# Down projection of a gated MLP as seven products of 2x2 blocks, with the sums of its weight blocks made ahead, in a one-core trunk kernel

## The chip, the cores and the metric

The kernel runs on one core of a Trainium2 chip. The metric is device time in microseconds (us) for one execution of the whole program. Five engines work side by side, each through its own queue, strictly in the queue's order: TensorE (PE in the profile; weight loads of the array are PEld), VectorE (DVE), ScalarE (ACT), GpSimd (POOL) and SyncE (SP), which here only issues DMAs. ACT issues a few DMAs too. An instruction waits at the head of its queue until the engines it depends on have signalled.

## What is computed

One decoder layer on x of 2048 tokens by 1024 channels, in float32: a token mixer of four head groups, then a gated channel mixer. The change lies in the channel mixer, which ends the program:

```python
D_MODEL, SEQ, D_FF = 1024, 2048, 2816
...
up, gate = split(rmsnorm(x, pre2) @ w_up)            # 1024 -> 2 x 2816
gate = causal_depthwise_conv(gate, width 3) + bias   # over tokens
h = gelu_tanh(gate) * up                             # 2048 x 2816, F in the kernel
out = x + rmsnorm(h @ w_down, post2)                 # 2816 -> 1024
```

(The names are shortened; the function is the reference's.) Float32 products are made of float16 ones: each operand is scaled by a power of two and split into a high and a low float16 part, and a product takes three matmuls, high by high, high by low and low by high.

## The kernel before

The stage in question is `stage_n` and, called from its end, `ffn_down`. P = 128 partitions, C = 512 columns, NF = 22 tiles of 128 hidden channels, NC = 4 blocks of 512 tokens, NSUB = 4 blocks of 128 tokens in each.

**Up projection.** `ffn_up(p, j, w)` makes hidden tile j for the pair p of token blocks (p = 0: tokens 0 to 1023, p = 1: the rest). It already uses seven products of 2x2 blocks (L1672, 7 x 12 = 84 matmuls of 128x512), with the outputs put together on ACT and DVE (L1675, L1685, L1689). The convolution and GELU follow on ACT and DVE (L1705 to L1708), the multiplication by `up` on POOL (L1709), and the tile goes to DRAM as `fD` (L1710). Its largest magnitude is taken on DVE (L1711, `mF`) in the *next* call, as `late`. Tiles are taken in the order (0, j), (1, j), (0, j+1), ..., and the built program interleaves neighbouring calls.

The weights of tile j+1 are prepared while tile j is multiplied. `up_weights` loads 1 MB (`raw`), takes the largest magnitude on DVE, spreads it over the partitions with an all-reduce on POOL (L1625), and makes the four differences and sums of blocks on POOL (L1626). `up_split` computes the scale on DVE (L220 to L222, L1649) and writes the high part on ACT (L1652) and the low part on DVE (L1653) into `Wup`. `down_max` reads tile j of the down weights (512 KB, `rd`) only to take its largest magnitude (`mD`, L1638).

**Between the projections.** `f_scale(p)` finds the scale of pair p's F with one all-reduce on POOL (L1723); for p = 0 the scale of the down weights comes from the same one.

**Down projection.** For the first block of 512 tokens, every hidden tile j loads its weights again (`weights`, 512 KB on ACT's DMA queue, L1751), splits them on ACT and DVE (L1753, L1754) into `Wd`, which then stays in SBUF, loads and splits F (`values`, L1759 to L1762) and adds 8 x 3 matmuls of 128x512 (L1768) into eight PSUM banks. The other three blocks go by 128 tokens, with two banks each. `out` scales, normalises, adds x and stores.

The order in each queue is fixed when the program is built, by a scheduler that lists instructions by priority; `issue_after` moves a group of instructions behind a given one.

Of the kernel before, what the change touches and what calls it, by code (L numbers as in the profile page):

```python
# [97 lines left out]
def _layout(inp):  # L98
# [41 lines left out]
class Trunk:  # L140
# [1430 lines left out]
    def stage_n(self):  # L1571
# [3 lines left out]
        self.fD = self.dram.tile([NF, P, T], F32, name="fD")  # L1575
        with ExitStack() as ctx:
            self.small = self.sn
            self.Wt.append(self.pool(ctx, "n_w").tile([P, 2, 7, C], F16, name="Wup1"))
# [3 lines left out]
            self.up, self.gb, self.F = two("up", [P, 2, C]), two("gb", [P, 2 * C + 2]), two("F", [P, 2, C])  # L1582
            self.rd = one("rd", [P, D])
# [72 lines left out]
    def ffn_up(self, p, j, w):  # L1656
# [57 lines left out]
    def f_scale(self, p, mark):

        nc, small = self.nc, self.sn
        self.small = small
        n = 2 if p else 3
        mm = small.tile([P, 6], F32, name="mm", bufs=2)
        nc.vector.tensor_reduce(out=mm[:, 0:2], in_=self.mF[:, 2 * p:2 * p + 2], axis=AX.X, op=ALU.max)  # L1720
        if p == 0:
            nc.vector.tensor_reduce(out=mm[:, 2:3], in_=self.mD, axis=AX.X, op=ALU.max)
        nc.gpsimd.partition_all_reduce(mm[:, 3:3 + n], mm[:, 0:n], P, RMAX)  # L1723
        with self.tc.issue_after(mark.ins):
            un, sc = self.pow2(mm[:, 3:3 + n], 14)
            if p == 0:
                nc.vector.tensor_copy(out=self.sd[:, 0:1], in_=un[:, 2:3])
                nc.vector.tensor_copy(out=self.sd[:, 1:2], in_=sc[:, 2:3])
            nc.vector.tensor_scalar(out=self.sf[:, 2 * p:2 * p + 2, 0], in0=un[:, 0:2], scalar1=self.sd[:, 0:1], scalar2=None, op0=ALU.mult)
            nc.vector.tensor_copy(out=self.sf[:, 2 * p:2 * p + 2, 1], in_=sc[:, 0:2])  # L1730

    def ffn_down(self):

        nc = self.nc
        with ExitStack() as ctx:
            wa = self.pool(ctx, "wa_d")
            Wd = [None] * 3 + [wa.tile([P, 2, D], F16, name=f"Wd{j}") for j in range(3, 18)]
            s0 = self.pool(ctx, "s0_d")
            early = [s0.tile([P, D], F32, name="wdr0"), s0.tile([P, 2, C], F32, name="fr0"), s0.tile([P, 3, 2, C], F16, name="f0")]
            wb = self.pool(ctx, "wb_d")  # L1740
            st = self.pool(ctx, "st_d", bufs=4)
            fp = self.pool(ctx, "f_d")
            self.row(fp, "post2")
# [3 lines left out]
            Wd = [wb.tile([P, 2, D], F16, name=f"Wd{j}") for j in range(3)] + Wd[3:] + [wb.tile([P, 2, D], F16, name=f"Wd{j}") for j in range(18, NF)]  # L1747

            def weights(j):
                r = early[0] if j < 3 else st.tile([P, D], F32, name="wdr", bufs=3)  # L1750
                nc.scalar.dma_start(out=r, in_=self.A["w_dn"][j])  # L1751
                W = Wd[j]
                nc.scalar.activation(out=W[:, 0], in_=r, func=AF.Copy, scale=sd[:, 1:2])  # L1753
                self.mark = nc.vector.scalar_tensor_tensor(out=W[:, 1], in0=r, scalar=sd[:, 1:2], in1=W[:, 0], op0=ALU.mult, op1=ALU.subtract)  # L1754

            def values(c, j):
                e = c == 0 and j < 3
                r = early[1][:, j % 2] if e else st.tile([P, C], F32, name="fr")
                nc.sync.dma_start(out=r, in_=self.fD[j][:, c * C:(c + 1) * C])  # L1759
                f = early[2][:, j] if e else fp.tile([P, 2, C], F16, name="f", bufs=NF + 5)  # L1760
                nc.scalar.activation(out=f[:, 0], in_=r, func=AF.Copy, scale=sf[:, c, 1:2])
                nc.vector.scalar_tensor_tensor(out=f[:, 1], in0=r, scalar=sf[:, c, 1:2], in1=f[:, 0], op0=ALU.mult, op1=ALU.subtract)  # L1762
                return f

            def mms(ps, f, i, n, j):
                sl, ns = slice(i * P, (i + 1) * P), slice(n * C, (n + 1) * C)
                for k, (a, b) in enumerate(((0, 0), (0, 1), (1, 0))):
                    nc.tensor.matmul(ps, lhsT=f[:, a, sl], rhs=Wd[j][:, b, ns], start=j == 0 and k == 0, stop=j == NF - 1 and k == 2)  # L1768

            def out(c, i, ps):  # L1770
                r = slice(c * C + i * P, c * C + (i + 1) * P)
                x = fp.tile([P, D], F32, name="xo", bufs=3)
                nc.scalar.dma_start(out=x, in_=self.x2[r])
                o = fp.tile([P, D], F32, name="od", bufs=2)
                nc.scalar.activation(out=o[:, 0:C], in_=ps[0], func=AF.Copy, scale=sf[:, c, 0:1])
                nc.vector.tensor_scalar(out=o[:, C:], in0=ps[1], scalar1=sf[:, c, 0:1], scalar2=None, op0=ALU.mult)  # L1776
                jk = fp.tile([P, D], BF16, name="jk", bufs=1)
                ss = small.tile([P, 2], F32, name="nss")
                nc.scalar.activation(out=jk, in_=o, func=AF.Square, accum_out=ss[:, 0:1])
                self.small = small  # L1780
                self.rsqrt(ss[:, 1:2], ss[:, 0:1], 1.0 / D, EPS)
# [6 lines left out]
            for j in range(NF):  # L1788
                weights(j)
                f = values(0, j)  # L1790
                if j == 8:
                    self.f_scale(1, self.mark)
                for i in range(NSUB):
                    for n in range(2):
                        mms(ps[i][n], f, i, n, j)
# [37 lines left out]
```

## Time and profile before

| | |
|---|---|
| median of 3 runs | 3024.64 us (3021.18 to 3032.18) |
| the profiled execution | 3021.11 us, span 3019.3 us, mean granted clock 0.943 |
| PE busy | 2746.7 us, 91% of the span |
| DVE, ACT, POOL busy | 1726.0, 1038.3, 802.9 us (57%, 34%, 27%) |
| up stage, steady, one hidden tile j (168 matmuls) | 36.69 us |
| last matmul of the up projection ends | 2528.3 us |
| first matmul of the down projection | 2542.55 us |
| down projection | 2112 matmuls |

The span runs from the first to the last instruction that the profile shows; the profiled execution's own time is 1.8 us longer. Busy shares are averages over the program; a stage is read from its own rows. A row of a timeline gives start, duration, engine, line and operation, and in brackets how long the engine had been idle and what released it.

### The profile page before, as it was taken

How to read it: one execution, taken by the hardware profiler on the slowest of the kernel's cores; microseconds unless marked ns; L12 is line 12 of the kernel's file. 1: busy time of each engine (PE TensorE's matmuls, PEld its weight loads, DVE VectorE, ACT ScalarE, POOL GpSimd, SP SyncE). 2: the span in 40 equal slices, each digit the busy share in tenths (PEclk: the TensorE clock that was granted, in tenths of full speed). 3: DMA queues.
4: the chain of work that ended last, by engine and by line, in shares of the span. 5: the costliest groups of instructions: out<-in, count | busy, mean ns of one | idle time of the engine just before them, and what ended most of it. 6: DMA issues, size and time to landing. Idle time of an engine off the chain costs nothing.

```text
span 3019.3 us, 45043 instructions
## 1 busy us (share of the span) xinstructions
PE 2746.7 (91%) x17401; PEld 1655.2 (55%) x17401; DVE 1726.0 (57%) x3517; ACT 1038.3 (34%) x1844; POOL 802.9 (27%) x979
## 2 busy tenths in 40 slices
PE   5998998999978997899966779999999997999998
PEld 2455776777757885676744424444444443444443
DVE  7645674767766554677864566666666665513021
ACT  5433222444532224466662322222233223412020
POOL 2432221323333331123333332322222221010110
PEclk9998998999988998899987989999999998999999
DMA  9522333345543384574433311122111214623120
GB/s 264 123 62 79 87 92 96 93 103 139 132 113 85 93 218 152 133 169 125 121 85 92 91 56 63 70 74 73 70 70 70 72 70 158 213 91 105 42 87 22
DMA packets 341400, 313.70 MB, mean 104 GB/s; under 512 B 217600, under 2 KB 271232, under 8 KB 338368
## 3 DMA queue, kind: packets, MB, share of 16 engines
q1 hardware_dynamic: 265856, 238.42, 27.9%
q10 hardware_dynamic: 75328, 72.39, 8.1%
q8 instruction: 137, 2.24, 0.3%
q14 instruction: 79, 0.65, 0.1%
HBM read 187.86 MB, written 89.56 MB: 92 GB/s over the span
## 4 chain that ended last, share of the span: by engine, by line
PE 61%; DVE 14%; issue 9%; DMA 7%; ACT 4%; POOL 3%; SPq 1%; ACTq 0%; POOLq 0%; DVEq 0%
PE psd L1768 10%; PE psb L1672 9%; PE psc L1672 5%; PE psa L1672 5%; PE psf L298 2%; PE psf L299 2%; PE psf L300 2%; DVE Wup L1653 2%; PE psf L308 1%; PE psf L310 1%; PE psf L309 1%; PE psb L662 1%; PE pss L1253 1%; PE pso L1415 1%; PE psb L682 1%
## 5 line engine op out<-in xcount | busy, mean ns | idle before, releaser
L1672 PEld LDWEIGHTS <-Wup 128*128 128x128 f16 x3696 | 362.8, 99 | 518.0 <-issue 61.2
L1768 PE MATMUL psd<-Wd,f 128*128 128x512 f16 x2112 | 460.9, 381 | 20.9 <-ACT Wd L1753 20.0
L1768 PEld LDWEIGHTS <-f 128*128 128x128 f16 x2112 | 207.6, 98 | 274.2 <-issue 19.1
L1672 PE MATMUL psa<-V,Wup 128*128 128x512 f16 x1056 | 254.7, 385 | 34.2 <-ACT Wup L1652 17.0
L1672 PE MATMUL psb<-T,Wup 128*128 128x512 f16 x792 | 189.7, 382 | 17.9 <-ACT T L1567 13.5
L1675 DVE SCALAR_TENSOR_TENSOR up<-psb,wm,X 128x512 f32<-128x512 f32 x88 | 65.9, 749 | 214.4 <-PE psb L1672 214.2
L308 PE MATMUL psg<-Wo,yt 128*128 128x256 f16 x512 | 145.4, 284 | 29.8 <-DMA yt<-hl 25.2
L1685 ACT ACTIVATE X<-psa,wm 128x512 f32<-128x512 f32 x44 | 30.2, 687 | 389.0 <-DVE up L1675 387.2
L298 PE MATMUL psf<-U,hi_fm 128*128 128x256 f16 x576 | 162.4, 282 | 0.0
L299 PE MATMUL psf<-U,hi_fm 128*128 128x256 f16 x576 | 162.3, 282 | 0.0
L300 PE MATMUL psf<-U,lo_fm 128*128 128x256 f16 x576 | 162.0, 281 | 0.0
L310 PE MATMUL psg<-Wo,yt 128*128 128x256 f16 x512 | 144.3, 284 | 5.4 <-DMA yt<-hl 5.4
L309 PE MATMUL psg<-Wo,yt 128*128 128x256 f16 x512 | 145.4, 284 | 0.0
L1776 DVE TENSOR_SCALAR od<-psd,sf 128x512 f32<-128x512 f32 x16 | 12.0, 750 | 232.0 <-PE psd L1768 227.5
L308 PE MATMUL psf<-hi_fv,U 128*128 128x256 f16 (+1 forms) x512 | 136.2, 275 | 1.4 <-DVE gt L873 1.4
L309 PE MATMUL psf<-lo_fv,U 128*128 128x256 f16 (+1 forms) x512 | 136.1, 274 | 1.1 <-DVE lo_fv L286 1.1
L310 PE MATMUL psf<-hi_fv,U 128*128 128x256 f16 (+1 forms) x512 | 136.5, 274 | 0.0
L1371 DVE TENSOR_REDUCE fmx<-psf 128x1 f32<-128x512 f32 (+3 forms) x160 | 95.8, 606 | 56.3 <-PE psf L1368 39.9
L1709 POOL TENSOR_TENSOR F<-F,up 128x1024 f32<-128x1024 f32 x44 | 103.8, 2359 | 81.4 <-ACT F L1708 74.1
L1672 PE MATMUL psc<-V,Wup 128*128 128x512 f16 x528 | 121.1, 379 | 0.0
L1405 ACT ACTIVATE fP<-psf,ln2k 128x512 f32<-128x512 f32 (+3 forms) x160 | 98.3, 626 | 65.6 <-PE psf L1403 26.6
L1415 PE MATMUL pso<-FV,fhl 128*128 128x129 f16 x1088 | 99.8, 227 | 15.3 <-POOL fhl L1409 7.6
(458 smaller groups left out, 6157.7 us busy)
## 6 DMA issues: line engine op xcount, KB each, us to landing
raw<-in_w_up SPq DMA_DIRECT2D x22, 1024.0 KB
fD<-F SPq DMA_DIRECT2D x44, 512.0 KB
fr<-fD SPq DMA_DIRECT2D x88, 256.0 KB
rd<-in_w_dn SPq DMA_DIRECT2D x22, 512.0 KB
wdr<-in_w_dn ACTq DMA_DIRECT2D x22, 512.0 KB
zin<-zR SPq DMA_DIRECT2D x80, 128.0 KB
ka<-kA ACTq DMA_DIRECT2D x40, 256.0 KB
wst<-in_w_cm SPq DMA_DIRECT2D x17, 512.0 KB
```

What stands on the lines that cost most here:

```text
L298: nc.tensor.matmul(ps[:, sl], lhsT=hi[:, k, n0:n0 + nn], rhs=uh[:, k, sl], start=k == 0, stop=False)
L299: nc.tensor.matmul(ps[:, sl], lhsT=hi[:, k, n0:n0 + nn], rhs=ul[:, k, sl], start=False, stop=False)
L300: nc.tensor.matmul(ps[:, sl], lhsT=lo[:, k, n0:n0 + nn], rhs=uh[:, k, sl], start=False, stop=k == KT - 1)
L308: nc.tensor.matmul(ps, lhsT=uh[:, k, sl], rhs=hi[:, k, n0:n0 + nn], start=k == 0, stop=False)
L309: nc.tensor.matmul(ps, lhsT=uh[:, k, sl], rhs=lo[:, k, n0:n0 + nn], start=False, stop=False)
L310: nc.tensor.matmul(ps, lhsT=ul[:, k, sl], rhs=hi[:, k, n0:n0 + nn], start=False, stop=k == KT - 1)
L1371: nc.vector.tensor_reduce(out=mx[:, i, b:b + 1], in_=ps[:, :n], axis=AX.X, op=ALU.min)
L1405: nc.scalar.activation(out=e[:, o:], in_=ps[:, o:], func=AF.Exp, scale=-1.0, bias=self.ln2k)
L1415: nc.tensor.matmul(po[i // 2][:, i % 2 * 129:i % 2 * 129 + 129], lhsT=h[:, n, i * P:(i + 1) * P], rhs=self.V2[:, s, hp], start=s == 0 and ...
L1672: nc.tensor.matmul(ps, lhsT=W[:, a, n, ks], rhs=rhs[u](b, k), start=first and k == 0 and i == 0, stop=k == 3 and i == 2, skip_group_check= ...
L1709: nc.gpsimd.tensor_tensor(out=t, in0=t, in1=up.rearrange("p c n -> p (c n)"), op=ALU.mult)
L1768: nc.tensor.matmul(ps, lhsT=f[:, a, sl], rhs=Wd[j][:, b, ns], start=j == 0 and k == 0, stop=j == NF - 1 and k == 2)
```

## The change

The down projection is written as seven products of 2x2 blocks as well: the hidden tiles are paired (j with j + 11), the two halves of the 1024 output columns, and the two token blocks of a pair p. A step (p, i, j) takes 128 tokens of each block of the pair, seven combinations of F and seven of the weights, and 7 x 3 = 21 matmuls into seven PSUM banks. There are 2 x 4 x 11 = 88 steps. `out` adds the seven banks up into four quarters.

- `down_max` becomes `down_sums`: for each of the 11 pairs it loads 1 MB of down weights, takes the largest magnitude, makes four differences on POOL in place and stores them to DRAM as `dT`. It is called 11 times, with the tiles j = 4 to 14 of the up stage, after `ffn_up(1, j)`.
- `d_scale`, with an all-reduce of its own, takes over the down weights' scale; `f_scale` keeps one scale for the pair.
- F goes to `fD` in two stores of 256 KB, laid out by 128-token blocks.
- The last `ffn_up` calls change places: (0, 20), (0, 21), (1, 20), (1, 21).
- `weights(j)` loads 0.75 MB of `w_dn` and 1 MB of `dT`, on SP's queue, into two buffers or into the space of `Wd8`, `Wd9`, `Wd10`. `values` loads F for one step into `X`, makes four 128x128 sums on POOL, and splits the 896 columns on ACT and DVE into `O`. Both run three steps ahead of the matmuls, the first three steps in memory that the first pair's up projection has left.

```diff
     def down_sums(self, j, mark):
+        d = self.rd
+        nc.sync.dma_start(out=d.rearrange("p s n -> p (s n)"), in_=self.A["w_dn"][j])
         with self.tc.issue_after(mark.ins):
-            nc.vector.tensor_reduce(out=self.mD[:, j:j + 1], in_=d, axis=AX.X, op=ALU.max, apply_absolute_value=True)
+            nc.vector.tensor_reduce(out=self.mD[:, j:j + 1], in_=d.rearrange("p s n -> p (s n)"), axis=AX.X, op=ALU.max, apply_absolute_value=True)
+        for o, a, b in ((1, 0, 1), (0, 3, 0), (3, 3, 1), (2, 3, 2)):
+            nc.gpsimd.tensor_tensor(out=d[:, o], in0=d[:, a], in1=d[:, b], op=ALU.subtract)
+        nc.sync.dma_start(out=self.dT[j], in_=d)
...
     def stage_n(self):
-            for j in range(2, NF):
...
+            for j in range(2, NF - 1):
+                W[j + 1] = self.up_weights(j + 1)
                 mark = self.ffn_up(0, j, W[j])
+                W[j + 1] = self.up_split(j + 1, W[j + 1], mark)
+                if j < NF - 2:
+                    mark = self.ffn_up(1, j, W[j])
+                    if 4 <= j < 4 + NF // 2:
+                        self.down_sums(j - 4, mark)
+                    if j == 5 + NF // 2:
+                        self.d_scale(mark)
+            self.ffn_up(0, NF - 1, W[NF - 1])
+            self.f_scale(0, self.ffn_up(1, NF - 2, W[NF - 2]))
+            self.ffn_up(1, NF - 1, W[NF - 1])
             self.late()
...
+    def d_scale(self, mark):
+        nc.vector.tensor_reduce(out=mm[:, 0:1], in_=self.mD, axis=AX.X, op=ALU.max)
+        nc.gpsimd.partition_all_reduce(mm[:, 1:2], mm[:, 0:1], P, RMAX)
...
     def ffn_down(self):
+            def weights(j):
+                r, W = raw[(0, 1, 0, 2, 3, 0, 1, 2, 0, 1, 0)[j]], Wd[j]
+                nc.sync.dma_start(out=r[0], in_=self.A["w_dn"][j][:, C:].rearrange("p (s n) -> p s n", s=3))
+                nc.sync.dma_start(out=r[1], in_=self.dT[j])
+                for o, x in ((slice(0, 3), r[0]), (slice(3, 7), r[1])):
+                    nc.scalar.activation(out=W[:, 0, o], in_=x, func=AF.Copy, scale=sd[:, 1:2])
+                    self.mark = nc.vector.scalar_tensor_tensor(out=W[:, 1, o], in0=x, scalar=sd[:, 1:2], in1=W[:, 0, o], op0=ALU.mult, op1=ALU.subtract)
+
+            def values(n, p, i, j):
+                x, o = X[n % 3], O[n % 4]
+                nc.sync.dma_start(out=x[:, 0:4].rearrange("p (h s) t -> p h (s t)", h=2), in_=self.fD[:, j, :, p, i].rearrange("h p n -> p h n"))
+                for d, a, b, op in ((4, 0, 2, ALU.add), (5, 4, 1, ALU.subtract), (6, 1, 0, ALU.subtract), (7, 3, 5, ALU.subtract)):
+                    nc.gpsimd.tensor_tensor(out=x[:, d], in0=x[:, a], in1=x[:, b], op=op)
+                nc.scalar.activation(out=o[:, 0], in_=x[:, 1:8], func=AF.Copy, scale=sf[:, p, 1:2])
+                nc.vector.scalar_tensor_tensor(out=o[:, 1], in0=x[:, 1:8], scalar=sf[:, p, 1:2], in1=o[:, 0], op0=ALU.mult, op1=ALU.subtract)
+                return o
...
+            for n in range(lead):
+                prepare(n)
+            for n, (p, i, j) in enumerate(steps):
+                prepare(n + lead)
...
+                for b, (a, w) in zip(ps, ((0, 0), (4, 6), (2, 1), (5, 3), (3, 4), (6, 2), (1, 5))):
+                    for k, (x, y) in enumerate(((0, 0), (0, 1), (1, 0))):
+                        nc.tensor.matmul(b, lhsT=o[:, x, a], rhs=W[:, y, w], start=j == 0 and k == 0, stop=j == H - 1 and k == 2)
+                if j == H - 1:
+                    out(p, i, ps)
```

POOL's queue in one step of the up stage before: the block sums of the next up weights, and F's multiplication behind them (ISA rows are the all-reduce and the switches of POOL's library on either side of it).

```order
L1626 TENSOR_TENSOR S<-raw 128x512
L1625 ISA
L1625 ISA wm<-wm 128x1
L1626 ISA
L1626 TENSOR_TENSOR raw<-raw 128x512
L1626 TENSOR_TENSOR S<-raw 128x512
L1626 TENSOR_TENSOR S<-raw,S 128x512
L1709 TENSOR_TENSOR F_19222<-F_19222,up_19206 128x1024
```

POOL's queue after the change: the end of the same step with `down_sums`, and the later step in which `d_scale` falls (L1716 is F's multiplication, L1644 the four differences, L1728 the all-reduce of `d_scale`).

```order
L1629 TENSOR_TENSOR S<-raw,S 128x512
L1644 TENSOR_TENSOR rd<-rd 128x512 x4
L1716 TENSOR_TENSOR F_19237<-F_19237,up_19229 128x1024
...
L1629 TENSOR_TENSOR S<-raw,S 128x512
L1644 TENSOR_TENSOR rd<-rd 128x512
L1728 ISA
L1728 ISA md<-md 128x1
L1644 ISA
L1644 TENSOR_TENSOR rd<-rd 128x512 x3
L1716 TENSOR_TENSOR F_19237<-F_19237,up_19229 128x1024
```

In each of these steps four differences, and once an all-reduce with two library switches, have come between the block sums and F's multiplication. The two rows of calls behind F's multiplication are as before.

DVE's queue at the same place, after the change; the names and their order are those of before (L1719 was L1711, L1660 was L1653).

```order
L1682 SCALAR_TENSOR_TENSOR up_19221<-psb,wm,X 128x512
L1719 TENSOR_REDUCE mF<-F_19237 128x2
L221 TENSOR_SCALAR p_1_22658<-wm 128x1
L1682 SCALAR_TENSOR_TENSOR gb_19225<-psb,wm,X 128x512
L222 TENSOR_SCALAR p_1_22658<-p_1_22658 128x1
L1682 SCALAR_TENSOR_TENSOR gb_19217<-psc,wm,gb_19217 128x512
L223 RECIPROCAL p_1_22658<-p_1_22658 128x1
L1656 TENSOR_TENSOR wm<-p_1_22658,ug 128x1
L1713 SCALAR_TENSOR_TENSOR F_19233<-gb_19217,pc,F_19233 128x1024
L1714 SCALAR_TENSOR_TENSOR F_19233<-gb_19217,pc,F_19233 128x1024
L1660 SCALAR_TENSOR_TENSOR Wup_19209<-raw,p_1_22658,Wup_19209 128x2048
```

Nothing moved here: the maximum of F stands where it stood, ahead of the scale and the split of the next up weights.

SP's queue after the change, at the end of the up stage: the loads up to the weights of the first step (`st`), and the last stores of F (L1781 and L1782 are the two loads of `weights`, L1790 is that of `values`).

```order
L1718 DMA fD<-F_19237 128x4x128 x2
L1781 DMA Wd_24398<-in_w_dn 128x1536
L1782 DMA Wd_24398<-dT_19191 128x2048
...
L1781 DMA Wd_24398<-in_w_dn 128x1536
L1718 DMA fD<-F_19233 128x4x128 x2
L1781 DMA Wd_24423<-in_w_dn 128x1536
L1782 DMA Wd_24423<-dT_19193 128x2048
L1781 DMA Wd_24419<-in_w_dn 128x1536
L1782 DMA Wd_24419<-dT_19194 128x2048
L1782 DMA Wd_24398<-dT_19196 128x2048
L1781 DMA st_24389<-in_w_dn 128x1536
L1782 DMA st_24390<-dT_19190 128x2048
```

The weights of the pairs 1, 6, 3 and 4 are loaded ahead of those of pair 0, with which the first matmul works; before, the weights came on ACT's queue, tile by tile in the order of their use.

One more count from PE's queue: between the ten matmuls that wait for a Wup's low part and the first that uses the following Wup stand 160 matmuls in a steady step (the ten counted in), before and now; ahead of the last Wup it was 160 too and is 102 now, since (0, 21) follows (0, 20) directly.

## Rows read from the trace of the kernel before

**Rows 1.** The page's chain of waits by line, shares of the span.

```profile
PE psd L1768 10%; PE psb L1672 9%; PE psc L1672 5%; PE psa L1672 5%; PE psf L298 2%; PE psf L299 2%; PE psf L300 2%; DVE Wup L1653 2%; PE psf L308 1%; PE psf L310 1%; PE psf L309 1%; PE psb L662 1%; PE pss L1253 1%; PE pso L1415 1%; PE psb L682 1%
```

**Rows 2.** Windows: busy by engine (x instructions), PEclk granted clock, DMA share, GB/s.

```profile
2400.00:2436.69 36.69, 36.44 (x170) 16.34 (x168) 23.67 (x24) 10.37 (x10) 10.69 (x11) 1.00 0.20 72
2549.00:2559.00 10.00, 7.03 (x32) 3.03 (x31) 5.12 (x5) 5.79 (x7) 0.37 (x1) 1.00 0.99 361
2760.00:3010.00 250.00, 250.00 (x1159) 113.19 (x1157) 46.62 (x61) 39.22 (x60) 24.72 (x17) 1.00 0.21 70
```

**Rows 3.** Timeline, PE, two successive waits in the up stage.

```profile
2414.08 2.33 PE L1672 MATMUL psa<-V,Wup 128*128 128x512 f16 x10 [0.25 <-DVE Wup L1653]
...
2450.77 2.33 PE L1672 MATMUL psa<-V,Wup 128*128 128x512 f16 x10 [0.25 <-DVE Wup L1653]
```

**Rows 4.** Timeline, POOL, one step of the up stage.

```profile
2400.98 2.35 POOL L1709 TENSOR_TENSOR F<-F,up 128x1024 f32<-128x1024 f32 x1
...
2419.09 1.27 POOL L1626 TENSOR_TENSOR S<-raw 128x512 f32<-128x512 f32 x1 [2.66 <-DMA raw<-in_w_up]
2426.21 0.38 POOL L1625 PARTITION_ALL_REDUCE wm<-wm  x1 [5.84 <-DVE gb L1675]
2433.64 1.25 POOL L1626 TENSOR_TENSOR raw<-raw 128x512 f32<-128x512 f32 x1 [7.05 <-issue]
...
2436.32 1.26 POOL L1626 TENSOR_TENSOR S<-raw,S 128x512 f32<-128x512 f32 x1
2437.54 2.35 POOL L1709 TENSOR_TENSOR F<-F,up 128x1024 f32<-128x1024 f32 x1
```

**Rows 5.** Timeline, DVE, the same step and the end of the one before.

```profile
2405.03 1.21 DVE L1711 TENSOR_REDUCE mF<-F 128x2 f32<-128x1024 f32 x1
...
2441.72 1.21 DVE L1711 TENSOR_REDUCE mF<-F 128x2 f32<-128x1024 f32 x1
...
2444.38 0.14 DVE L1649 TENSOR_TENSOR wm<-p,ug 128x1 f32<-128x1 f32 x1
...
2447.16 1.28 DVE L1707 SCALAR_TENSOR_TENSOR F<-gb,pc,F 128x1024 f32<-128x1024 f32 x1
2448.36 2.35 DVE L1653 SCALAR_TENSOR_TENSOR Wup<-raw,p,Wup 128x2048 f16<-128x2048 f32 x1
```

**Rows 6.** Timeline, ACT, the same step.

```profile
2444.57 1.24 ACT L1705 ACTIVATE F<-gb,pc 128x1024 f32<-128x1024 f32 x1 [1.98 <-DVE wm L1649]
2445.71 1.99 ACT L1652 ACTIVATE Wup<-raw,p 128x2048 f16<-128x2048 f32 x1
2447.61 1.56 ACT L1652 ACTIVATE Wup<-S,p 128x1536 f16<-128x1536 f32 x1
```

**Rows 7.** Timeline, PE, from the up to the down projection.

```profile
2525.59 2.75 PE L1672 MATMUL psc<-V,Wup 128*128 128x512 f16 x12
2542.55 3.57 PE L1768 MATMUL psd<-Wd,f 128*128 128x512 f16 x8 [14.21 <-ACT Wd L1753]
2547.08 3.61 PE L1768 MATMUL psd<-Wd,f 128*128 128x512 f16 x16 [0.95 <-DVE Wd L1754]
2551.93 5.34 PE L1768 MATMUL psd<-Wd,f 128*128 128x512 f16 x24 [1.24 <-ACT Wd L1753]
2561.79 1.44 PE L1768 MATMUL psd<-Wd,f 128*128 128x512 f16 x3 [4.52 <-ACT Wd L1753]
```

**Rows 8.** Timeline, DVE: the same split without and with F's multiplication on POOL.

```profile
1684.82 1.81 DVE L1653 SCALAR_TENSOR_TENSOR Wup<-S,p,Wup 128x1536 f16<-128x1536 f32 x1
...
2451.29 3.45 DVE L1653 SCALAR_TENSOR_TENSOR Wup<-S,p,Wup 128x1536 f16<-128x1536 f32 x1
```

**Rows 9.** Timeline, the end of the program.

```profile
3004.78 5.34 PE L1768 MATMUL psd<-Wd,f 128*128 128x512 f16 x24
...
3013.01 1.28 DVE L1782 SCALAR_TENSOR_TENSOR od<-od,nss,r_post 128x1024 f32<-128x1024 f32 x1 [0.66 <-POOL nss L231]
3014.33 1.22 DVE L1783 TENSOR_TENSOR xo<-xo,od 128x1024 f32<-128x1024 f32 x1
```

More of the change, by code (lines that the diff above doesn't have):

```diff
@@ L1581, in stage_n @@
             self.X = one("X", [P, C])
-            self.up, self.gb, self.F = two("up", [P, 2, C]), two("gb", [P, 2 * C + 2]), two("F", [P, 2, C])
-            self.rd = one("rd", [P, D])
+            self.gb, self.up = zip(*((one(f"gb{i}", [P, 2 * C + 2]), one(f"up{i}", [P, 2, C])) for i in range(2)))
+            self.F = two("F", [P, 2, C])
             self.nup = 0
@@ L1717, in f_scale @@
         self.small = small
[L1718 to L1723, printed above, removed]
-        with self.tc.issue_after(mark.ins):
[L1725 to L1730, printed above, removed]
+        mm = small.tile([P, 2], F32, name="mm", bufs=2)
@@ L1732, in ffn_down @@
     def ffn_down(self):
         nc = self.nc
+        H = NF // 2
         with ExitStack() as ctx:
[L1736 to L1741, printed above, removed]
@@ L1746, in ffn_down @@
             sd, sf = self.sd, self.sf
-            Wd = [wb.tile([P, 2, D], F16, name=f"Wd{j}") for j in range(3)] + Wd[3:] + [wb.tile([P, 2, D], F16, name=f"Wd{j}") for j in range(18, NF)]
+            view = lambda j, o, n: Wd[j].rearrange("p s m n -> p (s m n)")[:, 2 * o * C:2 * (o + n) * C].bitcast(F32).rearrange("p (s n) -> p s n", s=n)
+            raw = [(st[0][:, 0:3], st[1])] + [(view(j, 4, 3), view(j, 0, 4)) for j in (10, 9, 8)]
             def weights(j):
[L1750 to L1781, printed above, removed]
-                nc.vector.scalar_tensor_tensor(out=o, in0=o, scalar=ss[:, 1:2], in1=self.pr["post2"], op0=ALU.mult, op1=ALU.mult)
-                (nc.vector if c == NC - 1 and i == NSUB - 1 else nc.gpsimd).tensor_tensor(out=x, in0=x, in1=o, op=ALU.add)
-                nc.sync.dma_start(out=self.out[r], in_=x)
@@ L1786, in ffn_down @@
-            bank = lambda: ps_.tile([P, C], F32, name="psd")
-            ps = [[bank() for n in range(2)] for i in range(NSUB)]
[L1788 to L1795, printed above, removed]
-                    if j == NF - 1:
-                        out(0, i, ps[i])
```

112 lines of the change are left out of this document (83 added, 29 removed).

## The prediction

> **What bounds the kernel now.** I read the page's chain of waits first: PE's matmuls lead it, and those of the down projection (L1768) are the largest group, 10% of the span [rows 1]. The windows then show how full PE is. In the body of the down projection it is busy for the whole of 250 us, with 1159 matmuls at the full granted clock, so a matmul counts 0.2157 us there. In a steady step of the up stage it is busy for 36.44 of 36.69 us [rows 2]. Both stages are therefore bound by PE; matmuls taken away are gained, and anything that holds PE up is lost in full.
>
> How near the up stage is to being held up is seen in the timelines of one step. PE already waits 0.25 us in every step for the low part of the next weights, from one wait to the next in 36.69 us [rows 3]. POOL's block sums stand behind the second of two library switches, 5.84 us idle ahead of the all-reduce and 7.05 us behind it, and F's multiplication comes right behind them, ending at 2437.54 + 2.35 = 2439.89 [rows 4]. The maximum of F on DVE starts at 2441.72, 1.83 us later; in the step before, 2405.03 against 2400.98 + 2.35 = 2403.33, it is 1.70 [rows 4, 5]. Behind that maximum DVE has the last sums of the gate, the scale, and the split, with no slack: the scale ends at 2444.52, ACT starts at 2444.57, DVE's split starts at 2448.36 and ends when PE goes on [rows 3, 5, 6]. So 1.8 us is all that POOL may be late at this place.
>
> **Matmuls.** 88 steps of 21 are 1848, against 2112. 264 fewer at 0.2157 us: **-57.0 us**.
>
> **Sums in the up stage.** In 11 steps four differences of 128x512 come between the block sums and F's multiplication. From the first block sum behind the switch to F's start is (2437.54 - 2433.64) / 3 = 1.30 us each [rows 4], so 5.2 us. Less the slack of 1.8, F's maximum is 3.4 us late; what is queued behind it on DVE is late by the same, then ACT's high part, then PE. The next weights' load, its maximum and all-reduce start from the same split, so the next step finds the same 1.8 us again and nothing is caught up. 11 x 3.4 = **+37.5 us**. Bounds: 0, if another 3.4 us of slack lay in DVE's work behind the maximum, where the rows show none, and 11 x 5.2 = 57.
>
> The new loads and stores (1 MB each way) take no part of the path: the steps hold 72 GB/s [rows 2], and nobody waits for the stores until the down projection. DVE's maximum over 1 MB replaces two over 512 KB, at the same total.
>
> **The scale of the down weights.** In one of these steps `d_scale`'s all-reduce stands among the four differences. Its two switches and itself are 5.84 + 0.38 + 7.05 = 13.3 us [rows 4], with the slack spent: +13.3. PE is then idle for over 16 us. After an idle time of 14.21 us the eight matmuls that followed took 3.57 us, 0.43 each, half the granted clock, and after 0.95 and 1.24 us they ran at the full one [rows 7]; I put 8 to 13 slow matmuls, 2 us, on each idle time over 4 us. **+15.3 us**.
>
> By the Trainium skill (GPSIMD Engine Reference, section 2.1, instruction dispatch) the first call to a newly loaded kernel pays an instruction load of about 6 us. Priced by that page alone, for both switches, the term would be about 14.4 us and the sum 0.9 lower; the rows' 5.84 and 7.05 agree with it to a fifth, and I use the rows.
>
> **The last tiles.** With (0, 21) directly behind (0, 20), the weights of tile 21 are wanted 102 matmuls after PE's restart instead of 160: 22.0 us. What they need ends, counted from the restart at 2414.08, with the last block sum (2437.58: 23.5 us) [rows 3, 4]; then F's multiplication (2.35), its maximum (1.21), the scale (about 0.6) and ACT's high part (1.99) [rows 4 to 6]: 29.7. PE waits 7.7, less about 0.8 of small waits on the way, and runs slow for 2: **+9 us** (6 to 11).
>
> **From up to down.** Before, PE's last up matmul ends at 2528.3; then it is idle for 14.21, 0.95, 1.24 and 4.52 us [rows 7]. After:
> - Ahead of the add that frees a bank for the last up products, DVE has three splits of `O` and one of `Wd1`. A split of 896 columns lies between those of 512 and 1024, up to 1.28 [rows 5]; three of 1.15 and one of 1.81 [rows 8] are 5.3. PE waits 5 and runs slow for 2: +7 (0 to 10).
> - The first matmul needs `Wd0`, whose loads stand on SP behind the pairs 6, 3 and 4. Up to `st0` that is 0.75 + 0.5 + 1.75 + 1.75 + 1 + 0.75 = 6.5 MB (6.8 million bytes); while loads crowd, 361 GB/s flow [rows 2]: 18.9 us, and 1.56 for ACT [rows 6]. These loads begin about when the last up matmuls run. I take 20 us idle against 14.2: +6 (0 to 12).
> - The next waits, for `Wd0`'s low parts (1.81 and 2.35) and the late second half, are about 10 us in all, against 6.7: +3 (-3 to 8).
>
> Together **+16 us** (-3 to 30).
>
> **The down projection in step.** A step is 21 x 0.2157 = 4.53 us. POOL's four sums of 128x128 are about 0.46 each (from 1.27 at 512 columns and 2.35 at 1024, a straight line) [rows 4], 1.84; ACT and DVE take less than 2 and 1.3. That fits. In the first 11 steps the weights come on top: DVE 1.81 + 2.35 + 1.15 = 5.3. Here rows show something else: the split of 1.81 us took 3.45 while F's multiplication ran on POOL for 1.83 of it [rows 4, 8], so that such DVE and POOL work adds up: 7.15 us a step, 79 for eleven; by DMA 2.25 MB a step are 6.5 us, 72. They begin about 12 us ahead of the last up matmul, so end some 67 us behind it; PE wants the eleventh at 20 + 10 + 10 x 4.53 = 75. Hidden, by 8 us: **0** (to 29, below).
>
> The rule behind this is in the Trainium skill (GPSIMD Engine Reference, section 1, specifications): GpSimd shares its SBUF interfaces with VectorE, and contends with DVE instructions that have two SBUF inputs. The trace agrees, with 3.45 against 1.81. Without the rule DVE alone would need 58 us, and the sum would be the same.
>
> **Banks and tail.** Seven group boundaries, each with one spare bank instead of up to six: 0 to 1 us each, I take +2. At the end `out` normalises two rows of 1024 per partition, so DVE's 1.28 and 1.22 [rows 9] stand twice: **+2.5**.
>
> **Sum.** 3021.1 - 57.0 + 37.5 + 15.3 + 9 + 16 + 2 + 2.5 = 3046.4. The profiled execution lies 3.5 below the median of its runs, which spread over 11; I leave that in the range, and predict **3047 us**, 0.7% slower.
>
> **Rivals.**
> - *The end of the up stage costs nothing* (about the same time). The loads for the first steps begin while the last pair is multiplied, so the start may be no later than before, and the last tiles' wait may fall into time that was lost anyway: 3046 - 9 - 16 = 3021. For it: before, some 26 us are lost there (the 2112 matmuls at 0.2157 ending at 3010.1 would have begun at 2554.5 [rows 2, 7, 9]). Against: the weights of pair 0 are fifth in the queue. Chance 0.19.
> - *The differences on POOL fit in* (faster). If F's maximum may be late without holding the split, the 37.5, 13.3 and 2 go: 2994. It decides at 5.2 us of slack where two steps show 1.70 and 1.83. Half of that slack would give 3020. Chance 0.08.
> - *The first eleven steps starve* (slower still). If the splits of the weights run at 7.15 us a step from the first matmul on, 2.6 x 11 = 29 are added: 3075. For it: DVE and POOL do add up; against: the 8 us worked out above. Part of it is likelier than all. Chance 0.13.
> - *The forecast*, 3030 to 3062: 0.60.
>
> **Chances and range.** From no change a measurement here tells about 0.5%, 15 us. Faster by more than that: 0.09 (the second rival, and the tail of the first). Within it: 0.20. Slower: 0.71 (the forecast, less its lower end, and the third). 3018 to 3068 leaves out most of the second rival and half of the third, some 0.15 to 0.2.
>
> **What the profile would show.** Right: 11 steps of about 40 us in the up stage, with F's multiplication some 5 us behind the block sums and PE released by DVE's `Wup`; one step longer by some 13 us more; a wait of about 7 us before tile 21; a first down matmul about 20 us behind the last up matmul, released by ACT's `Wd` after a DMA; 1848 matmuls, full from then on. Wrong: steps of 36.7 us with the four differences in them (the slack was misread), a first down matmul after less than 14 us (the queue was), or waits for `O` or `Wd` in the middle of the down projection.

## The result, and the profile after

The changed kernel takes **3046.27 us** (median of 4 runs, 3043.36 to 3047.45) against 3022.91 for the kernel before in the same comparison (4 runs, 3016.20 to 3032.18): a ratio of 1.0068, interval 1.0048 to 1.0088. It is 0.7% slower with 264 matmuls fewer. The prediction was 3047 us. Each of its terms holds to 3.2 us; four came out larger than said and four smaller, and these errors cancel.

Earlier stages vary from one execution to another: the same PE restart in the up stage comes between 1818.09 and 1841.69 us in the thirteen profiled executions of this document. So profiled executions are compared below by the **rest**: the time from that restart (1826.78 before, 1827.61 after; two steps ahead of the first step with differences) to the end of the span. The rest is 1192.5 us before and 3045.4 - 1827.61 = 1217.8 after: +25.3.

The page after, the costliest groups of the down projection on PE, POOL and DVE (engine, operation, tile, count | busy us, mean ns of one | idle time ahead):

```profile
L1846 PE MATMUL psd<-Wd,O 128*128 128x512 f16 x1848 | 404.1, 382 | 28.5 <-ACT Wd L1784 23.3
...
L1792 POOL TENSOR_TENSOR X<-X 128x128 f32<-128x128 f32 x352 | 221.8, 653 | 113.8 <-DMA X<-fD 91.2
...
L1794 DVE SCALAR_TENSOR_TENSOR O<-X,sf,O 128x896 f16<-128x896 f32 x88 | 135.9, 1563 | 147.4 <-ACT O L1793 147.4
```

1848 matmuls, as counted. Over the whole down projection PE lost only 28.5 us to waits, 23.3 of them for ACT's high parts of `Wd`; these are the waits at its start. The window of what follows them (us; busy time and count of PE, PEld, DVE, ACT and POOL; granted clock, DMA share, GB/s):

```profile
2640.00:3031.00 391.00, 389.96 (x1799) 176.39 (x1799) 195.97 (x164) 125.34 (x134) 275.93 (x366) 1.00 0.32 109
```

PE is full and at the full granted clock, as in the body before [rows 2]. DVE (196 of 391 us) and POOL (276) are far busier than before and hold nothing up. So the 57 us were really saved; they were lost again ahead of this window, but for 3.5 us at the very end. Timeline, PE, restarts in the up stage, then the step with the scale's all-reduce:

```profile
2102.14 2.33 PE L1679 MATMUL psa<-V,Wup 128*128 128x512 f16 x10 [0.38 <-DVE Wup L1660]
...
2135.93 2.75 PE L1679 MATMUL psb<-T,Wup 128*128 128x512 f16 x12 [1.67 <-DVE p L222]
2139.95 0.60 PE L1679 MATMUL psa<-V,Wup 128*128 128x512 f16 x2 [1.27 <-ACT Wup L1659]
...
2142.96 2.33 PE L1679 MATMUL psa<-V,Wup 128*128 128x512 f16 x10 [0.38 <-DVE Wup L1660]
...
2304.83 2.33 PE L1679 MATMUL psa<-V,Wup 128*128 128x512 f16 x10 [0.38 <-DVE Wup L1660]
...
2352.21 4.10 PE L1679 MATMUL psb<-T,Wup 128*128 128x512 f16 x12 [15.26 <-DVE p L222]
2356.22 0.60 PE L1679 MATMUL psa<-V,Wup 128*128 128x512 f16 x2
...
2359.23 2.33 PE L1679 MATMUL psa<-V,Wup 128*128 128x512 f16 x10 [0.38 <-DVE Wup L1660]
```

A step is 2142.96 - 2102.14 = 40.82 us where it was 36.69 [rows 3], and the one with `d_scale` 54.40. Ten such steps are 39.95 to 40.82, mean 40.39. POOL and DVE in the first of the two show why:

```profile
2125.07 1.27 POOL L1629 TENSOR_TENSOR S<-raw,S 128x512 f32<-128x512 f32 x1
2126.29 5.31 POOL L1644 TENSOR_TENSOR rd<-rd 128x512 f32<-128x512 f32 x4
2131.56 2.34 POOL L1716 TENSOR_TENSOR F<-F,up 128x1024 f32<-128x1024 f32 x1
```
```profile
2133.94 1.22 DVE L1719 TENSOR_REDUCE mF<-F 128x2 f32<-128x1024 f32 x1 [4.07 <-POOL F L1716]
...
2140.55 2.35 DVE L1660 SCALAR_TENSOR_TENSOR Wup<-raw,p,Wup 128x2048 f16<-128x2048 f32 x1
```

Before, F's product had ended 1.8 us ahead when DVE came to its maximum [rows 4, 5]; now DVE stands idle for 4.07 us and starts 0.04 us behind POOL's end (2131.56 + 2.34 = 2133.90). From the maximum on, the chain up to the low part of `Wup` is as it was: 6.61 us from one to the other, 6.64 before [rows 5]. In the later step POOL has the all-reduce between the first difference and the other three, with a switch on either side:

```profile
2328.84 1.26 POOL L1644 TENSOR_TENSOR rd<-rd 128x512 f32<-128x512 f32 x1
2336.43 0.38 POOL L1728 PARTITION_ALL_REDUCE md<-md  x1 [6.33 <-issue]
2343.95 3.94 POOL L1644 TENSOR_TENSOR rd<-rd 128x512 f32<-128x512 f32 x3 [7.14 <-issue]
```

PE from tile 21 to the down projection, which answers to [rows 7]:

```profile
2536.24 1.03 PE L1679 MATMUL psa<-V,Wup 128*128 128x512 f16 x2 [7.11 <-ACT Wup L1659]
...
2592.48 5.12 PE L1679 MATMUL psb<-T,Wup 128*128 128x512 f16 x12 [5.38 <-DVE up L1682]
2597.44 2.75 PE L1679 MATMUL psc<-V,Wup 128*128 128x512 f16 x12
...
2621.15 0.59 PE L1846 MATMUL psd<-Wd,O 128*128 128x512 f16 x1 [20.95 <-ACT Wd L1784]
...
2625.85 11.76 PE L1846 MATMUL psd<-Wd,O 128*128 128x512 f16 x41 [4.12 <-DVE Wd L1785]
2639.99 0.81 PE L1846 MATMUL psd<-Wd,O 128*128 128x512 f16 x3 [2.38 <-ACT Wd L1784]
2641.84 8.45 PE L1846 MATMUL psd<-Wd,O 128*128 128x512 f16 x31 [1.04 <-DVE Wd L1785]
```

Three waits stand here: 7.11 for tile 21, 5.38 for a PSUM bank behind DVE's work, 20.95 for `Wd0`. The 12 matmuls behind the second take 5.12 us instead of 2.75.

### The profile page after: what moved, and what is told of

It is laid out like the page before. It is cut to its first block, busy times and chain, and to the rows that moved or that the text cites. A ratio compares the mean times of both kernels' runs of the same rounds, so it can differ in the third digit from the quotient of the medians.

```text
span 3045.4 us, 45223 instructions
## 1 busy us (share of the span) xinstructions
PE 2701.1 (89%) x17137; PEld 1629.1 (53%) x17137; DVE 1834.2 (60%) x3536; ACT 1081.7 (36%) x1844; POOL 1125.8 (37%) x1391
## 4 chain that ended last, share of the span: by engine, by line
PE 56%; DVE 15%; issue 9%; DMA 8%; POOL 7%; ACT 3%; SPq 1%; ACTq 0%; POOLq 0%; DVEq 0%
PE psd L1846 13%; PE psb L1679 5%; PE psa L1679 3%; PE psc L1679 3%; POOL rd L1644 2%; PE psf L299 2%; PE psf L300 2%; PE psf L301 2%; DVE Wup L1660 1%; PE psf L309 1%; PE psf L311 1%; PE psf L310 1%; DVE mF L1719 1%; PE pss L1254 1%; PE psb L663 1%
## 5 line engine op out<-in xcount | busy, mean ns | idle before, releaser
L1846 PE MATMUL psd<-Wd,O 128*128 128x512 f16 x1848 | 404.1, 382 | 28.5 <-ACT Wd L1784 23.3
L1846 PEld LDWEIGHTS <-O 128*128 128x128 f16 x1848 | 181.9, 98 | 250.7 <-issue 35.6
L1792 POOL TENSOR_TENSOR X<-X 128x128 f32<-128x128 f32 x352 | 221.8, 653 | 113.8 <-DMA X<-fD 91.2
L1794 DVE SCALAR_TENSOR_TENSOR O<-X,sf,O 128x896 f16<-128x896 f32 x88 | 135.9, 1563 | 147.4 <-ACT O L1793 147.4
L1793 ACT ACTIVATE O<-X,sf 128x896 f16<-128x896 f32 x88 | 90.6, 1040 | 212.4 <-PE psd L1846 125.2
L1410 POOL TENSOR_TENSOR fhl<-fP,fhl 128x512 f16<-128x512 f32 (+3 forms) x52 | 59.3, 1141 | 171.8 <-ACT fhl L1408 124.3
```

Of the source, the lines that this page charges most:

```text
L1792: nc.gpsimd.tensor_tensor(out=x[:, d], in0=x[:, a], in1=x[:, b], op=op)
L1794: nc.vector.scalar_tensor_tensor(out=o[:, 1], in0=x[:, 1:8], scalar=sf[:, p, 1:2], in1=o[:, 0], op0=ALU.mult, op1=ALU.subtract)
L1846: nc.tensor.matmul(b, lhsT=o[:, x, a], rhs=W[:, y, w], start=j == 0 and k == 0, stop=j == H - 1 and k == 2)
```

## The experiments

Each ratio is against runs of the kernel before that were made beside it on the same chip; experiments 5 to 8 are from another chip than the others. "One run" has no interval, and of those the rest is what counts. Every rest comes from one profiled execution.

| kernel | us | before | ratio (95%) | rest, us |
|---|---|---|---|---|
| changed kernel | 3046.27 | 3022.91 | 1.0068 (1.0048 to 1.0088) | 1217.8 |
| differences behind F | 3038.47, one run | 3034.1 | | 1198.7 |
| two ahead of F, two behind | 3034.97, one run | 3034.1 | | 1198.7 |
| one all-reduce less | 3048.71, one run | 3034.1 | | 1205.2 |
| both (first and third) | 3017.02 | 3034.1 | 0.9951 (0.9932 to 0.9969) | 1183.5 |
| and `rd` loaded last | 2995.76 | 3027.4 | 0.9886 (0.9849 to 0.9924) | 1166.8 |
| changed kernel, again | 3055.21 | 3027.4 | 1.0092 (1.0062 to 1.0122) | 1223.3 |
| and old tile order | 2991.45 | 3027.4 | 0.9869 (0.9835 to 0.9904) | 1159.6 |
| or weights by use | 2993.24 | 3027.4 | 0.9882 (0.9841 to 0.9923) | 1159.5 |
| both of these | 2988.14 | 3028.02 | 0.9862 (0.9834 to 0.9890) | 1159.6 |
| by use, late scale | 2991.36 | 3028.02 | 0.9875 (0.9841 to 0.9910) | 1161.7 |
| by use, no sums of `X` | 2973.02, one run | 3028.02 | | 1151.3 |

**1. Differences behind F's product** (`fm` is F's multiplication on POOL).

```diff
+        with self.tc.issue_after(self.fm.ins):
             for o, a, b in ((1, 0, 1), (0, 3, 0), (3, 3, 1), (2, 3, 2)):
```

> One edit: the four differences of down_sums stand behind F's multiplication on POOL instead of ahead of it. Theory (order: F's maximum is late, and DVE holds the next split back behind it): the steps fall from 40.4 us back to about 36.7, 11 x 3.7 = 41 us come back; some 3005 us. The step with the scale's all-reduce still costs 13 to 14 us. Rival (load: the steps are longer because POOL, the DMA queues or the SBUF interfaces carry more): the same work is done in the same steps, so they stay near 40 us and the time near 3046.

The rest fell by 19.1 us, half of what was expected. DVE's wait for F shrank, from 3.2 to 4.1 us in a step of the changed kernel to 0 to 1.7 here, but nine of the ten steps without `d_scale` are 38.0 to 39.4 us, not 36.7. Something else had taken its place.

**2. Two differences ahead of F, two behind.** As in 1, with the first two left outside of the `with`.

> One edit: two of the four differences stand ahead of F's multiplication, two behind it. Theory (slack of 1.7 to 1.8 us): two differences make F 2.6 us late, 0.9 us beyond the slack, so a step is about 37.6 us and 11 of them cost 10 us; some 3015 us. Rival (the cost goes with the number of differences ahead of F, without slack): half of 3.7, steps of 38.5 us, some 3026.

The rest fell by 19.1 us again: the total of the rival, but by neither account, since steps are of two kinds. Of the ten without `d_scale`, six take 37.5 to 38.2 us, near the 37.6 that the slack asks for, and four 39.5 to 40.5. In the six, the block sums use `raw` 5.0 to 5.8 us behind its issue, in the four 7.1 to 7.7. Timeline, SP and then POOL, of two neighbours:

```profile
2020.75 0.35 SPq L1640 DMA_DIRECT2D rd<-in_w_dn  x1
2021.62 0.33 SPq L1625 DMA_DIRECT2D raw<-in_w_up  x1
...
2059.34 0.34 SPq L1640 DMA_DIRECT2D rd<-in_w_dn  x1
2061.86 0.33 SPq L1625 DMA_DIRECT2D raw<-in_w_up  x1
```
```profile
2029.34 1.27 POOL L1629 TENSOR_TENSOR S<-raw 128x512 f32<-128x512 f32 x1 [5.33 <-DMA raw<-in_w_up]
...
2066.93 1.27 POOL L1629 TENSOR_TENSOR S<-raw 128x512 f32<-128x512 f32 x1 [2.69 <-DMA raw<-in_w_up]
```

Where the load of `rd` (1 MB) goes out 0.87 us ahead of that of `raw` (1 MB), `raw` is used 2029.34 - 2021.62 = 7.7 us behind its issue, and the step is 40.24 us; where it goes out 2.52 us ahead, 5.1 and 37.59. The distance alone does not sort the steps: in the other three long ones, too, `rd` went out 2.4 to 2.5 us ahead, and why `raw` was late there is not shown. The suspicion was this: the later the differences end, the later the next `rd` is loaded, and it runs into the load that the step waits for. Experiment 5 tests it.

**3. One all-reduce less.** `d_scale` is taken out; `f_scale(0)` reduces the down weights' maximum as a second column.

```diff
-                    if j == 5 + NF // 2:
-                        self.d_scale(mark)
...
+        if p == 0:
+            nc.vector.tensor_reduce(out=mm[:, 1:2], in_=self.mD, axis=AX.X, op=ALU.max)
+        nc.gpsimd.partition_all_reduce(mm[:, 2:2 + n], mm[:, 0:n], P, RMAX)
```

> One edit: d_scale is gone; the maximum of the down weights goes through the all-reduce of f_scale(0), as before the change. Theory: in the step where PE waited 15.3 us, the two switches of POOL's library (6.3 and 7.1 us) and the all-reduce go, the wait falls to that of the other steps and the slow matmuls behind it go too; 15 us less, some 3031. Rival: the switches are paid somewhere else (the next all-reduce finds its library cold anyway), and less than 5 us are saved.

The rest fell by 12.6 us, and no step of 54 us is left (all eleven are 40.0 to 40.9). The term is `d_scale`'s, as said.

**4. Both, 1 and 3.**

> Both edits: the differences behind F's multiplication, and no all-reduce of its own for the down weights' scale. Theory: the two costs add, 41 + 15 = 56 us, some 2990 us, 1.1% faster than the kernel before the change; the up stage is then that of before except for the last tiles. Rival: with the up stage shorter, stores of F and of dT or POOL's later differences collide with the next block sums and 10 us or more stay; over 3000.

The rest fell by 34.3 us instead of 56, about 12.6 + 19.1, and the kernel is 0.5% faster than before. Timeline of one step, SP and POOL:

```profile
2095.32 0.34 SPq L1638 DMA_DIRECT2D rd<-in_w_dn  x1
2096.07 0.33 SPq L1623 DMA_DIRECT2D raw<-in_w_up  x1
```
```profile
2103.55 1.27 POOL L1627 TENSOR_TENSOR S<-raw 128x512 f32<-128x512 f32 x1 [5.31 <-DMA raw<-in_w_up]
```

`raw` is used 7.48 us behind its issue, against 5.45 in a step of the changed kernel (2102.11 to 2107.56), where `rd` goes out 7 us earlier. POOL's block sums and F are late by that, so that DVE waits 0.92 us for F again in this step; the differences run into DVE's work behind them, and one DVE row of 1.28 us [rows 5] takes 2.26:

```profile
2128.84 2.26 DVE L1712 SCALAR_TENSOR_TENSOR F<-gb,pc,F 128x1024 f32<-128x1024 f32 x1 [1.31 <-ACT F L1711]
```

Whether the cause was the load or this sharing with POOL was the next question.

**5. `rd` loaded behind `raw`** (on 4; `rl` is the load of `raw`).

```diff
                 W[j + 1] = self.up_weights(j + 1)
+                if 5 <= j < 5 + NF // 2:
+                    self.down_sums(j - 5, mark)
...
+        with self.tc.issue_after(self.rl.ins):
             nc.sync.dma_start(out=d.rearrange("p s n -> p (s n)"), in_=self.A["w_dn"][j])
```

> Both edits of the run e3_both, and one more: the 1 MB read of the down weights is issued behind the read of the next up weights instead of right ahead of it. Theory (what stays of e3_both's steps, 38.9 us against 36.7, is the late landing of the up weights, 7.4 us behind their issue, which shifts the block sums by 2.5 us and the differences into DVE's next work): the up weights land within 5 us, the steps come to 36.7 to 37.0 and some 22 us are gained on e3_both. Rival (the differences themselves, on the SBUF interfaces that POOL shares with DVE): the steps stay above 38 us wherever the read stands.

The two restarts, the loads and the first block sum of one step:

```profile
2086.42 2.33 PE L1679 MATMUL psa<-V,Wup 128*128 128x512 f16 x10 [0.25 <-DVE Wup L1660]
...
2123.10 2.33 PE L1679 MATMUL psa<-V,Wup 128*128 128x512 f16 x10 [0.24 <-DVE Wup L1660]
```
```profile
2123.07 0.34 SPq L1623 DMA_DIRECT2D raw<-in_w_up  x1
2123.46 0.42 SPq L1639 DMA_DIRECT2D rd<-in_w_dn  x1
```
```profile
2128.06 1.27 POOL L1627 TENSOR_TENSOR S<-raw 128x512 f32<-128x512 f32 x1 [2.62 <-DMA raw<-in_w_up]
```

Steps are 36.68 us (the longest 37.2), `raw` is used 4.99 us behind its issue, and DVE waits for F in none of them. The rest falls by another 16.7 us, and the kernel is 1.1% faster than before. The same four differences still run on POOL in every one of these steps, so the sharing was a consequence of the late load and not the cause. All that the up stage had lost to the differences and to `d_scale` is back: the eleven steps take 404.3 us, against 424.2 in 4 and 11 x 36.69 = 403.6 before. Whether `rd` on another queue would have done as well was not tried.

**6. The changed kernel once more**, on the chip of 5, 7 and 8.

> The changed kernel itself, on the chip of this call, as the measure for the others: 0.4 to 1.0% slower than the kernel before.

1.0092, with an interval that overlaps the first; 5 is 1.9% under it (2995.76 / 3055.21). Its rest is 5.5 us longer than in the first profile (the first down matmul comes after 22.89 us instead of 20.95, and the long steps are about 0.25 longer each), so differences of that size between two rests are not read by themselves. Those of 7 to 11 are little larger, and are read together with the waits.

**7. Old order of the last tiles** (on 5): (0, 20), (1, 20), (0, 21), (1, 21), with `f_scale(0)` behind them.

> e8_rd_last with the last tiles in the order of before the change, (0,20), (1,20), (0,21), (1,21), and the scale of the first pair behind them. Theory (the tiles' new order costs 7 to 8 us of waiting and 2 us of slow matmuls, and its early start of the down projection is lost behind the weights' loads anyway): no wait ahead of tile 21, a first down matmul 20 to 24 us behind the last up matmul as now, waits behind it longer by some 4 us; 5 to 9 us faster than e8_rd_last. Rival (the early F loads carry the start): the first down matmul comes 10 us or more later, and the time is that of e8_rd_last or more.

```profile
2562.48 0.58 PE L1840 MATMUL psd<-Wd,O 128*128 128x512 f16 x1 [24.36 <-ACT Wd L1778]
2564.37 2.72 PE L1840 MATMUL psd<-Wd,O 128*128 128x512 f16 x6 [1.31 <-ACT Wd L1778]
2570.14 9.40 PE L1840 MATMUL psd<-Wd,O 128*128 128x512 f16 x35 [3.05 <-DVE Wd L1779]
2588.99 1.44 PE L1840 MATMUL psd<-Wd,O 128*128 128x512 f16 x3 [9.45 <-ACT Wd L1778]
```

There is no wait ahead of tile 21 (8.63 us in 5). The wait for a bank (5.23 us in 5) is gone too, which was not expected: the scale now comes later, and DVE has no splits of `O` ahead of that add. With both gone, the time from the first restart to the end of the last up matmul is 17.3 us shorter. Behind it 10 come back: the four waits shown are 38.2 us in place of 30.1 in 5 (21.71, 4.81, 2.38, 1.24). The rest falls by 7.2, as expected. The medians of 5 and 7 are too near for the ratios to part them.

**8. Weights loaded in the order of use** (on 5): pair 0 goes to a buffer that is free early.

```diff
-                r, W = raw[(0, 1, 0, 2, 3, 0, 1, 2, 0, 1, 0)[j]], Wd[j]
+                r, W = raw[(1, 2, 3, 0, 1, 2, 3, 0, 2, 1, 0)[j]], Wd[j]
```

> e8_rd_last with the raw buffers of the down weights dealt out so that pair 0 has the one that is free first: pairs 0, 1 and 2 go through the space of Wd10, Wd9 and Wd8, pair 3 through st. Theory (the 21 us ahead of the first down matmul are the loads of pairs that are used later): that wait falls to 3 us or less, but the next ten pairs follow at the rate at which loads and splits can be had, 5.8 to 7 us a step against 4.5, so that most of it comes back as waits ahead of the next steps; 3 to 8 us faster in all. Rival (loads not in the way, the first split is late for another reason): the first wait stays at about 21 us. Other rival (nothing comes back): 18 us faster.

```profile
2551.21 4.97 PE L1841 MATMUL psd<-Wd,O 128*128 128x512 f16 x21
2560.26 1.44 PE L1841 MATMUL psd<-Wd,O 128*128 128x512 f16 x3 [4.08 <-ACT Wd L1779]
...
2589.16 25.27 PE L1841 MATMUL psd<-Wd,O 128*128 128x512 f16 x106 [4.82 <-ACT Wd L1779]
```
```profile
2558.63 1.57 ACT L1779 ACTIVATE Wd<-Wd,sd 128x1536 f16<-128x1536 f32 x1 [3.93 <-DMA Wd<-in_w_dn]
```
```profile
2545.00:2600.00 55.00, 41.21 (x147) 16.12 (x146) 42.73 (x27) 31.01 (x22) 28.97 (x29) 0.78 0.93 353
```

The first step follows the up projection without a wait: the 21 us were the queue's, as predicted. Nine later waits add up to 17.5 us against 30.1, but the matmuls among them run slow: the 85 up to the wait of 4.82 take 24.3 us, some 5 more than at the full clock. The rest falls by 7.3, and the medians of 5 and 8 do not part them either. DMA is busy for 0.93 of 2545 to 2600 here, at 353 GB/s; PE's mean granted clock there is 0.78.

**9. Both of these.**

> e9_old_tiles and e11_by_use together: the old order of the last tiles, and the raw buffers of the down weights dealt out by use. Theory (both start the down projection into the same limit, the work of preparing ten pairs): the gains don't add; the first wait is some 13 us, later waits come to more than 15 us, and the time is within 4 us of either. Rival (they add): 4 to 8 us less than either, 2985 us or less on the chip of the last call.

```profile
2543.54 14.55 PE L1840 MATMUL psd<-Wd,O 128*128 128x512 f16 x55 [14.88 <-ACT O L1787]
...
2576.86 19.14 PE L1840 MATMUL psd<-Wd,O 128*128 128x512 f16 x77 [16.08 <-ACT O L1787]
```
```profile
2559.09 1.83 POOL L1730 PARTITION_ALL_REDUCE mm<-mm  x1 [9.63 <-DVE mm L1727]
2573.23 5.83 POOL L1786 TENSOR_TENSOR X<-X 128x128 f32<-128x128 f32 x12 [12.31 <-issue]
```

The rest is 1159.6, that of each alone: the gains don't add. The two long waits are now for `O`, the sums and splits of F, and no longer for the weights. The second of them stands behind the second pair's scale on POOL, whose all-reduce and switches hold the sums of `X` up until 2573.23.

**10. The second scale later** (on 8): `f_scale(1)` at step 20 instead of 8, so that its switches (7.45 us ahead of the all-reduce and 8.76 behind it in 8) leave the first steps.

> e11_by_use with the all-reduce of the second pair's scale behind the preparation of step 20 instead of step 8's place in the code, where it stood right behind the last F on POOL and held POOL for 7.5 + 0.7 + 8.8 = 17 us while the first steps wanted their sums of X. Theory (those 17 us hold the first steps back, ACT waited 10.5 us for the sums and PE 4.8 us behind ACT): PE's waits ahead of step 11, 17.5 us, fall by 5 us or more, and the switch costs less than 3 us later, where three steps stand ready: 2 to 8 us faster than e11_by_use. Rival (the loads and splits of the weights are the limit, not POOL): the waits only move, the time is that of e11_by_use to 2 us.

The rest is 1161.7, no less than in 8 (1159.5). The wait of 4.82 us is gone, but those ahead of step 11 are no less in all, 18 us (0.3 to 3.9 each) against 17.5, and one of 2.49 ends at 2668, behind the switches' new place: the rival. Moving the switches out of the first steps gained nothing here; on 9, where they stand behind the longest wait, it was not tried.

**11. No sums of `X` in the first eleven steps** (on 8).

> e11_by_use without POOL's four sums of X in the first 11 steps (they are left out, so that the output is not the reference's). Theory (in the first 11 steps POOL's sums and DVE's splits get in each other's way: a sum takes 1.14 us instead of 0.46, a split of 1536 columns up to 2.3 instead of 1.81): DVE's splits take their free durations, 1.81, 2.35 and 1.15 us, and PE's waits ahead of step 11 fall from 17.5 us to 10 or less. Rival (DMA is the limit, 353 GB/s in these 55 us): the waits stay at 15 us or more.

```profile
2563.00 29.21 PE L1843 MATMUL psd<-Wd,O 128*128 128x512 f16 x126 [1.03 <-DVE Wd L1780]
```

The waits add up to 13.8 us, between what the two accounts asked for, and the rest falls by 8.2. The trace parts them by place. Up to the 55th matmul nothing changed: the waits there, up to the one shown, are 8.9 us here and in 8. In both, ACT waits there for loads of the weights, and two splits lie beside F's multiplication. Then 126 matmuls run without a wait, where 8 has the 4.82 us and slow matmuls: they take 29.2 us, the same ones some 36 in 8. In that stretch the splits do take their free durations (1.81, 2.35 and 1.14 us up to 2588), and nothing waits for POOL's switches and sums. From 2589 on the sums are there again, splits are slow beside them, and waits come back. So POOL, with switches and sums together, holds up the steps behind the first 55 matmuls, and not those ahead. How much of these first waits is the loads' alone stays open, since no run took the loads away.

## Why the prediction was right, step by step

- **Matmuls, -57.0:** shown. 1848, back to back at the full granted clock.
- **Differences, +3.4 a step:** +3.7 (mean of ten steps), 40.7 for eleven instead of 37.5. The mechanism is the one named: the slack of 1.8 us ahead of F's maximum is spent, and nothing is caught up. The rows behind the maximum kept their lengths; the term was 0.3 a step too small.
- **`d_scale`, +15.3:** the step is 54.40 - 40.39 = 14.0 longer. Its switches took 6.33 and 7.14 us where the sum had 5.84 and 7.05, 13.85 with the all-reduce. What was too large are the 2 us for slow matmuls: they came (12 in 4.10 us instead of 2.75) and cost nothing, since they fill the 1.27 us that PE waits at 2139.95 in an ordinary step. From the first of the 12 to the restart are 7.02 us, in an ordinary step 7.03. The rule of the Trainium skill (GPSIMD Engine Reference, section 2.1, instruction dispatch), about 6 us for a newly loaded kernel, agrees within a fifth on both sides again. Together the eleven steps lost 54.7 us against 52.8.
- **Last tiles, +9:** 7.11 of wait and some 1.6 of slow matmuls, 8.7.
- **From up to down, +16:** the bank's wait and its slow matmuls are 5.38 + 2.37 = 7.75 (7 said). In those 5.38 DVE has the three splits of `O`, but one sum of the convolution and the add itself in place of the split of `Wd1`, so that the near size is in part luck. The first down matmul comes after 20.95 us (20 said), +6.7 against [rows 7]; the waits behind it are 4.12 + 2.38 + 1.04 = 7.54 instead of 10, +0.8 for +3. This last was mis-sized. Experiment 8 shows the cause of the 20.95, experiment 7 that of the 7.11 and of the 5.38.
- **In step, 0:** no wait from 2641.84 on. POOL's 128x128 sums were put at 0.46 us and took 0.65 on average, and DVE's splits of 896 columns 1.56 instead of 1.15. DVE and POOL slow each other there, as one split was slowed in [rows 8]: where POOL has no sums, in experiment 11, such a split takes 1.14 us. The rule of sharing that the prediction names beside that row (GPSIMD Engine Reference of the Trainium skill, section 1, specifications) agrees. Cover was there: POOL 276 of 391 us, DVE 196.
- **Banks and tail, +2 and +2.5:** the first was too large, the second too small. From the end of the last up matmul to that of the last matmul are 432.55 us (2600.19 to 3032.74); less 1848 matmuls at 0.2157, PE lost 33.9 us there, 7.7 more than the 26.2 of before. The waits above are 6.7 + 0.8 of it, which leaves 0.2 for the banks. The span ends 12.7 us behind the last matmul, 3.5 more than before.

The measured terms add up to 54.7 + 8.7 + 7.75 + 7.7 + 3.5 - 57.0 = +25.4, against +25.3 in the rest and +25.3 in the prediction's sum. So close a sum is luck: the differences (by 3.2), the bank's wait, the first down matmul and the tail were put 5.7 us too low in all, and `d_scale`, the last tiles, the later waits (by 2.2) and the banks 5.6 too high.

The rivals: the second needed 5.2 us of slack, and DVE's idle 4.07 us ahead of `mF` refutes it. The third did not come: PE did not starve behind 2641.84. The first was half true in a way that I had not priced: experiments 7, 8 and 9 show that gains at the end of the up stage are given back in part, since the first steps behind it wait for the loads and then for POOL (experiments 8, 9 and 11).

What the prediction did not see is how much of the loss could be avoided. I read the differences as a cost of POOL's queue alone, and gave the loads no part of the path. That holds in the changed kernel, where `raw` is used 5.1 to 6.1 us behind its issue (4.9 to 6.1 before). But moved behind F, the differences still cost half of it, by way of SP's queue.

## What to carry to other kernels

A change that takes work off a full engine pays only if what prepares it fits into the slack of every in-order queue that it enters: measure that slack in a steady step (here 1.8 us on POOL), and multiply what exceeds it by the number of steps. When a queue's wait is removed and half of the loss stays, look at what the moved work now triggers, its DMAs first: a load that nobody waits for belongs behind the load that a step waits for. Gains at neighbouring places need not add (experiment 9), so each is priced with the other in place.

## What was not expected of the hardware

- Two loads of 1 MB on one queue, 0.4 to 1.6 us apart: the second was used 6.8 to 8.9 us behind its issue (21 loads in experiments 1, 2 and 4). With 2.4 to 2.5 us between them it was 5.0 to 5.8 in six cases and 7.1 to 7.5 in three (experiment 2), and 5.1 to 6.1 with 7 us between them (the changed kernel). When it went first, 0.4 us ahead of the other, it was used after 4.8 to 5.7 (experiment 5).
- POOL's 128x128 adds ran at 653 ns on average over the down projection. Where DVE's splits of weights overlap they are slower: 27 of them took 30.88 us from 2584.76 on in experiment 8, 1.14 each.
- A POOL library switch took 5.7 to 6.6 us ahead of an all-reduce and 6.7 to 7.7 behind it in the up stage, and 7.45 and 8.76 while DMA was busy for 0.93 of the time (experiment 8).
